# Down stage of a hybrid encoder block: four scratch half tiles are allocated ahead of the first four residual tiles

## The chip, the cores and the metric

The kernel runs on one core of a Trainium2 chip. The time of a run is device microseconds of that core, from one launch that computes the whole block. Beside the times there is one profiled execution, whose trace gives start, duration and releaser of each instruction on TensorE (PE for the matmuls, PEld for the weight loads), VectorE (DVE), ScalarE (ACT), GpSimd (POOL) and the DMA queues that SyncE (SP), ACT and POOL feed.

## The reference: what is computed

One layer of a streaming encoder over 1024 frames of width 1024, with 16 meta tokens ahead of them: a mixer (attention with a forgetting bias beside a diagonal state space model), and then a gated convolutional FFN, each with a residual, and a last norm.

```python
h = h + _mixer(_rmsnorm(h, norm_mix_g), ...)
xn  = _rmsnorm(h, norm_ffn_g)
hid = xn @ w_up                                   # 1024 -> 2 * 2816
conv = conv_b + sum(hp[:, j:j + L] * conv_w[j] for j in range(3))
val, gate = split(conv, 2)
h = h + (silu(gate) * val) @ w_down               # 2816 -> 1024: the Down stage
out = _rmsnorm(h, norm_final_g)[:, 16:]
```

Only the last product with its residual and the final norm lie behind the place of the change. The change leaves every number of it as it is.

## The kernel before, in words

**Up stage.** The hidden features come in 22 pairs of 128 rows, c = 0 to 21. For each pair the matmuls give a value half and a gate half; ACT and DVE apply the convolution into the tiles `ov` (value) and `og` (gate), 128 x 1024 floats each, ACT applies the silu to `og`, and one multiply (line 1313) puts the product into `ov`, which line 1320 stores to the DRAM array `a_d`. For c up to 20 the tiles are taken from two `ov` slots and one `og` slot, the multiply is POOL's and the store is issued by SP. For the last pair, c = 21, the two tiles are taken from the slots with the tag `h` (function `conv_out`), the multiply is DVE's and the store goes out on ACT's queue. The `hid` pool that holds all of these lies on the right side of SBUF and is closed at line 1755.

**Down stage.** `silu(gate) * val` times `w_down` is done as a Strassen-like scheme with seven products p = 0 to 6 on half matrices. The 11 row blocks of the inner dimension are dealt into four groups g = 0 to 3, of 2, 3, 3 and 3 blocks. `forms(p, j)` loads (SP, lines 1551, 1558, 1563) and splits the operands of one product and block into a high and a low part: a cast on ACT (line 1583) and a subtraction on POOL or DVE (line 137). `product(g, p, ...)` runs three matmuls (lines 1697 to 1699) per block into each of four PSUM banks, one for each token tile t = 0 to 3. Products 4, 5 and 6 add into the banks of products 0, 1 and 3 (`JOINS`): a bank is copied out after the first of the two, and again after the second. There are two sets of four banks, `mm, mm, mm, po` and `sp, tp, sp, tp`.

Of the first group, product 0 is copied out by ACT into four scratch half tiles `u2[0..3]`, 128 x 512 floats (line 1702). Product 4 goes on in the same four banks, and DVE adds these into the left halves of the residual tiles `hs[0..3]`, 128 x 1024 floats (line 1707). So PE may write product 4 into bank t only when ACT has copied it into `u2[t]`, and a later product may start on that bank only when DVE has added it into `hs[t]`. Products 1 and 5 of the first group are copied by ACT into `hs[4..7]` (line 1705). The residual rows themselves are loaded into `hs[0..3]` by four loads of 512 KB on SP's queue (line 1769), in a row; SP goes on with the operand loads of the next group behind them.

**Where the tiles lie.** After line 1755 the pool `down` is opened on the left side, and its tiles are laid out in the order in which they are asked for. They cover addresses that tiles of the closed pools held, and the framework makes the first write to a new tile wait for the last use of whatever lay there, tile by tile. In the built program, in bytes of a partition: the last pair's `ov_14620` lies at 164992 to 169104 and its `og_14527` at 169120 to 173232; the `ov` slots of the other pairs at 156800 to 160896 and 160896 to 164992; their `og` slot at 152704 to 156800. Before the change `hs0` to `hs3` fill 150240 to 166624 and `u20` to `u23` (the four `u2` tiles) 166624 to 174816.

The order of the instructions on each engine is set by a scheduler in the framework when the program is built. On each engine and each DMA queue they are issued in that order.

Of the kernel before, what the change touches and what calls it, by code (L numbers as in the profile page):

```python
# [9 lines left out]
F = mybir.dt.float32  # L10
# [9 lines left out]
P = 128  # L20
# [38 lines left out]
def block_kernel(ctx, tc, x, meta, xbt, x0t, g1t, w_q, w_k, w_v, w_f, w_u, w_g, b_f, w_ao, lam_d, bw_d, cw_d,  # L59
# [7 lines left out]
    def pool(stack, name, bufs=1, side=None, **k):  # L67
        return stack.enter_context(
            tc.tile_pool(name=name, bufs=bufs, side=side, reuse_waits="tile", **k))
# [1153 lines left out]
    u2 = [t_[:, i] for t_ in u2t for i in range(2)]  # L1223
# [532 lines left out]
    dn = pool(ctx, "down", side="left")  # L1756
# [3 lines left out]
    sq = dn.tile([P, 512], BF, name="sq")  # L1760
    eps = dn.tile([P, 1], F, name="eps")
    V.memset(eps, EPS)
    hs = [dn.tile([P, D], F, name=f"hs{c}") for c in range(4)]
    u2 = [dn.tile([P, 512], F, name=f"u2{c}") for c in range(4)]
    hs += [dn.tile([P, D], F, name=f"hs{c}") for c in range(4, KD)]
    small2 = [dn.tile([P, 4, 512], R, name=f"op{q}") for q in range(4, 6)]
    ops += [[t_[:, w] for w in range(4)] for t_ in small2]
# [420 lines left out]
```

## Time and profile before

| | us |
|---|---|
| median of 3 runs | 1429.18 (1429.15 to 1431.81) |
| the profiled execution, whole | 1430.84 |
| span of its trace | 1429.0 |
| PE busy | 1411.4 (99%) |
| POOL busy | 763.7 (53%) |
| DVE busy | 1068.9 (75%) |
| ACT busy | 708.8 (50%) |
| first matmul of the Down stage | 1205.42 |

A view "waits" lists who waited for whom on an engine, with the total, the number and the longest. "Timeline" lists instructions in order of time: start, duration, engine, line, operation, tiles, and in brackets the idle time of the engine just before and what ended it. "Windows" gives busy time by engine in stretches of the span, with the TensorE clock that was granted. "DMA" lists what was issued in a stretch, with the size and the median time from the issue to the landing. Times in the text are microseconds from the span's start.

### The profile page before, as it was taken

How to read it: one execution, taken by the hardware profiler on the slowest of the kernel's cores; microseconds unless marked ns; L12 is line 12 of the kernel's file. 1: busy time of each engine (PE TensorE's matmuls, PEld its weight loads, DVE VectorE, ACT ScalarE, POOL GpSimd, SP SyncE). 2: the span in 40 equal slices, each digit the busy share in tenths (PEclk: the TensorE clock that was granted, in tenths of full speed). 3: DMA queues.
4: the chain of work that ended last, by engine and by line, in shares of the span. 5: the costliest groups of instructions: out<-in, count | busy, mean ns of one | idle time of the engine just before them, and what ended most of it. 6: DMA issues, size and time to landing. Idle time of an engine off the chain costs nothing.

```text
span 1429.0 us, 26319 instructions
## 1 busy us (share of the span) xinstructions
PE 1411.4 (99%) x9607; PEld 1336.1 (94%) x9607; DVE 1068.9 (75%) x2048; ACT 708.8 (50%) x1381; POOL 763.7 (53%) x872
## 2 busy tenths in 40 slices
PE   8999999999999999999999999999999999999997
PEld 8999999988999999999889999999999999788886
DVE  7999888843667675665579977888887775698867
ACT  7647575423555565534645444444444445643444
POOL 1542267642456556327671344554546544798795
PEclk9999999999999999999999999999999999999999
DMA  8685744530157531087953246766644327864443
GB/s 301 174 200 144 157 111 137 165 119 31 53 156 168 127 103 56 24 302 274 195 169 125 68 126 162 201 183 173 167 127 133 98 83 274 282 209 129 132 94 118
DMA packets 93318, 216.17 MB, mean 151 GB/s; under 512 B 14802, under 2 KB 22610, under 8 KB 92804
## 3 DMA queue, kind: packets, MB, share of 16 engines
q1 hardware_dynamic: 74340, 170.28, 36.5%
q0 software_dynamic: 17696, 41.29, 15.0%
q10 hardware_dynamic: 1152, 2.91, 0.6%
q8 instruction: 76, 1.25, 0.4%
q14 instruction: 54, 0.44, 0.1%
HBM read 170.88 MB, written 71.71 MB: 170 GB/s over the span
## 4 chain that ended last, share of the span: by engine, by line
PE 94%; DMA 3%; ACT 1%; SPq 0%; DVE 0%; issue 0%; POOL 0%; POOLq 0%; DVEq 0%; ACTq 0%
PE mm L174 5%; PE mm L176 5%; PE mm L175 5%; PE sp L237 4%; PE sp L236 4%; PE sp L238 4%; PE tp L236 3%; PE mm L236 3%; PE tp L237 3%; PE mm L238 3%; PE tp L238 3%; PE mm L237 3%; PE po L966 3%; PE tp L920 2%; PE mm L1699 2%; PE mm L1697 2%
## 5 line engine op out<-in xcount | busy, mean ns | idle before, releaser
L174 PE MATMUL mm<-xhi,whi 128*128 128x342 f32 (+2 forms) x480 | 156.1, 325 | 0.0
L175 PE MATMUL mm<-xlo,whi 128*128 128x342 f32 (+2 forms) x480 | 155.3, 324 | 0.0
L176 PE MATMUL mm<-xhi,wlo 128*128 128x342 f32 (+2 forms) x480 | 154.7, 323 | 0.6 <-DMA wlo<-in_w_g_dram 0.6
L1313 POOL TENSOR_TENSOR ov<-ov,og 128x1024 f32<-128x1024 f32 x21 | 50.8, 2419 | 119.6 <-ACT og L1312 117.2
L137 DVE TENSOR_TENSOR sw<-sf,sw 128x512 fp32r<-128x512 f32 x72 | 73.4, 1019 | 45.8 <-ACT sw L1304 45.7
L1304 ACT CAST sw<-sf 128x512 fp32r<-128x512 f32 x72 | 44.9, 624 | 109.4 <-POOL sf L1451 79.9
L176 PEld LDWEIGHTS mm<-xhi,wlo 128*128 128x128 f32 x480 | 90.4, 188 | 1.6 <-DMA wlo<-in_w_g_dram 1.1
L174 PEld LDWEIGHTS mm<-xhi,whi 128*128 128x128 f32 x480 | 90.4, 188 | 1.1 <-issue 0.6
L175 PEld LDWEIGHTS mm<-xlo,whi 128*128 128x128 f32 x480 | 90.4, 188 | 0.4
L1451 POOL TENSOR_TENSOR sf<-raw,sf 128x512 f32<-128x512 f32 x36 | 62.8, 1744 | 38.8 <-DVE sw L137 38.6
L1451 POOL TENSOR_TENSOR sf<-raw 128x512 f32<-128x512 f32 x36 | 49.0, 1361 | 60.3 <-DVE sw L137 24.3
L238 PE MATMUL mm<-xhi,sw 128*128 128x258 f32 (+1 forms) x288 | 81.0, 281 | 0.0
L236 PE MATMUL mm<-xhi,sw 128*128 128x258 f32 (+1 forms) x288 | 80.8, 280 | 0.0
L237 PE MATMUL mm<-xlo,sw 128*128 128x258 f32 (+1 forms) x288 | 80.7, 280 | 0.0
L883 ACT ACTIVATE pt<-pt,mx 128x400 f32<-128x400 f32 (+5 forms) x72 | 53.1, 737 | 44.8 <-DVE mx L876 44.4
L1503 DVE SCALAR_TENSOR_TENSOR ov<-hv,cwt,ov 128x1024 f32<-128x1024 f32 x36 | 69.4, 1927 | 0.4 <-ACT ov L1501 0.4
L885 POOL TENSOR_SCALAR pt<-pt,mx 128x400 f32<-128x400 f32 (+5 forms) x72 | 51.8, 720 | 33.2 <-DVE mx L884 28.3
L1304 ACT CAST sw<-raw 128x512 fp32r<-128x512 f32 x70 | 43.0, 621 | 45.4 <-PE sp L238 23.5
L137 DVE TENSOR_TENSOR sw<-raw,sw 128x512 fp32r<-128x512 f32 x70 | 57.9, 830 | 4.2 <-ACT sw L1304 4.0
L137 DVE TENSOR_TENSOR tl<-tp,th 128x512 fp32r<-128x512 f32 (+1 forms) x80 | 50.7, 634 | 12.0 <-ACT th L923 11.3
L923 ACT CAST th<-tp 128x512 fp32r<-128x512 f32 (+1 forms) x80 | 43.4, 543 | 32.2 <-PE tp L920 22.5
L852 POOL CAST qz<-q 64x128 fp32r<-64x128 f32 (+1 forms) x72 | 20.2, 282 | 68.8 <-PE sp L871 67.4
(722 smaller groups left out, 5726.4 us busy)
## 6 DMA issues: line engine op xcount, KB each, us to landing
raw<-in_w_up_dram SPq DMA_DIRECT2D x44, 512.0 KB, 3.7
t_d<-in_w_dn_dram POOLq DMA_DIRECT2D x44, 256.0 KB, 7.1
wr<-t_d SPq DMA_DIRECT2D x44, 256.0 KB, 3.7
ar<-a_d SPq DMA_DIRECT2D x41, 256.0 KB, 4.3
a_d<-ov SPq DMA_DIRECT2D x18, 512.0 KB, 2.6
wr<-in_w_dn_dram SPq DMA_DIRECT2D x33, 256.0 KB, 3.8
t_d<-in_w_dn_dram SPq DMA_DIRECT2D x22, 256.0 KB, 4.3
t_d<-t_d SPq DMA_DIRECT2D x22, 256.0 KB, 4.8
```

The lines of the kernel that those rows point to most:

```text
L137: return eng.tensor_tensor(out_, src, hi.bitcast(F), ALU.subtract)
L174: yield PE.matmul(ps, whi[:, i, :], ahi[:, i], start=(i == 0), stop=False)
L175: yield PE.matmul(ps, whi[:, i, :], alo[:, i], start=False, stop=False)
L176: yield PE.matmul(ps, wlo[:, i, :], ahi[:, i], start=False, stop=(i == k - 1))
L236: PE.matmul(ps, a[0][:, i], bh, start=(i == 0 and not joins), stop=False, skip_group_check=True)
L237: PE.matmul(ps, a[0][:, i], bl, start=False, stop=False, skip_group_check=True)
L238: PE.matmul(ps, a[1][:, i], bh, start=False, stop=(i == kh - 1), skip_group_check=True)
L883: ends[:] = rd, S.activation(pt[:n, :kc], pt[:n, :kc], AF.Exp, bias=low, scale=-1.0, accum_out=nm[:n, 0:1])
L885: sc_.append(GP.tensor_scalar(pt[:n, :kc], pt[:n, :kc], nm[:n, 1:2], 1.0, ALU.mult, ALU.mult))
L1304: S.copy(hi, src)
L1451: sums.append(GP.tensor_tensor(f_, a, b, op))
L1503: V.scalar_tensor_tensor(out=o, in0=h_[:, j:SEQ + j], scalar=cwc(j, m), in1=o, op0=ALU.mult, op1=ALU.add)
```

## The change

Two lines trade places: the four `u2` tiles are asked for ahead of `hs[0..3]`.

```diff
     eps = dn.tile([P, 1], F, name="eps")
     V.memset(eps, EPS)
+    u2 = [dn.tile([P, 512], F, name=f"u2{c}") for c in range(4)]
     hs = [dn.tile([P, D], F, name=f"hs{c}") for c in range(4)]
-    u2 = [dn.tile([P, 512], F, name=f"u2{c}") for c in range(4)]
     hs += [dn.tile([P, D], F, name=f"hs{c}") for c in range(4, KD)]
     small2 = [dn.tile([P, 4, 512], R, name=f"op{q}") for q in range(4, 6)]
```

The addresses then are: `u20` to `u23` at 150240 to 158432, `hs0` at 158432 to 162528, `hs1` at 162528 to 166624, `hs2` at 166624 to 170720, `hs3` at 170720 to 174816. All else lies where it lay. The number in a tile's name is given in the order of asking, so `u20_14762` becomes `u20_14758`, and `hs0_14758` becomes `hs0_14762`.

No engine's instructions stand in another order than before; what differs is what some of them wait for. The names in brackets below are semaphores: `PE_49`, `DVE_49`, `Pool_49` and `Activation_49` count an engine's finished instructions, `DMAHW0_49` to `DMAHW7_49` landed transfers; on ACT and SP below `DMAHW5_49` is that of the last pair's store, `a_d<-ov_14620`.

On ACT, at the turn from the Up to the Down stage (`mm`, `po` are PSUM banks, `ar` and `wr` loaded operands, `xlo` a place for split ones):

```order
 L1361 ACTIVATE ov_14620<-mm_14677,cwt_9030 128x340 [waits PE_49]
 L1320 DMA a_d_81<-ov_14620 128x1024 [waits DVE_49]
-L1702 COPY u20_14762<-mm_14792 128x512 [waits DMAHW5_49,PE_49]
-L1702 COPY u21_14763<-mm_14793 128x512 [waits PE_49,Activation_49]
-L1702 COPY u23_14765<-po_14795 128x512
+L1702 COPY u20_14758<-mm_14792 128x512 [waits PE_49]
+L1702 COPY u21_14759<-mm_14793 128x512 [waits PE_49,Pool_49]
+L1702 COPY u23_14761<-po_14795 128x512
 L1583 CAST xlo_98<-ar_14870 128x512 [waits DMAHW1_49]
 L1583 CAST xlo_98<-wr_14868 128x512 [waits DMAHW0_49]
```

The first copy no longer waits for the store of the last pair; the second waits for POOL, which multiplied the pair before the last.

On SP's queue, at the residual loads, with the first operand loads of the next group behind them:

```order
-L1769 DMA hs0_14758<-h_d_80 128x1024 [waits DMAHW6_49]
-L1769 DMA hs1_14759<-h_d_80 128x1024 [waits DMAHW7_49]
-L1769 DMA hs2_14760<-h_d_80 128x1024 [waits DMAHW0_49]
-L1769 DMA hs3_14761<-h_d_80 128x1024 [waits DMAHW5_49,DMAHW1_49,DVE_49]
+L1769 DMA hs0_14762<-h_d_80 128x1024 [waits DMAHW6_49,DMAHW0_49]
+L1769 DMA hs1_14763<-h_d_80 128x1024 [waits DMAHW7_49,DMAHW5_49,DVE_49]
+L1769 DMA hs2_14764<-h_d_80 128x1024
+L1769 DMA hs3_14765<-h_d_80 128x1024 [waits DMAHW1_49]
 L1558 DMA ar_14916<-a_d_81 128x512 [waits DMAHW2_49]
 L1558 DMA ar_14918<-a_d_81 128x512 [waits DMAHW3_49,PE_49]
```

The wait for the last pair's store moves from the fourth residual load to the second; `hs2`, `hs3` and all operand loads stand behind it.

On DVE, the first adds of the Down stage, which read the banks and the residual tiles, and the splits behind them:

```order
-L1707 TENSOR_TENSOR hs0_14758<-hs0_14758,mm_14792 128x512 [waits DMAHW6_49,PE_49,Pool_49]
-L1707 TENSOR_TENSOR hs1_14759<-hs1_14759,mm_14793 128x512 [waits DMAHW7_49,PE_49]
-L137 TENSOR_TENSOR xlo_98<-ar_14886,xlo_98 128x512 [waits DMAHW5_49]
+L1707 TENSOR_TENSOR hs0_14762<-hs0_14762,mm_14792 128x512 [waits DMAHW0_49,DMAHW6_49,PE_49,Pool_49]
+L1707 TENSOR_TENSOR hs1_14763<-hs1_14763,mm_14793 128x512 [waits DMAHW5_49,DMAHW7_49,DVE_49,PE_49]
+L137 TENSOR_TENSOR xlo_98<-ar_14886,xlo_98 128x512
 L137 TENSOR_TENSOR xlo_98<-wr_14884,xlo_98 128x512 [waits DMAHW4_49]
 L137 TENSOR_TENSOR xlo_98<-ar_14894,xlo_98 128x512
 L137 TENSOR_TENSOR xlo_98<-wr_14892,xlo_98 128x512
```

The adds stand where they stood; the second one's residual tile now is the one that is loaded behind the store.

## The prediction

> **What bounds the kernel now.** The first part of the page and the view of PE's waits come first:
>
> ```profile
> PE 1411.4 (99%) x9607; PEld 1336.1 (94%) x9607; DVE 1068.9 (75%) x2048; ACT 708.8 (50%) x1381; POOL 763.7 (53%) x872
> ...
> PE mm L355 <- ACT uh L413: 5.3, 1, 5.3
> PE mm L1697 <- ACT u L1702: 2.7, 1, 2.7
> PE mm L176 <- DMA wlo<-in_w_g_dram: 0.6, 1, 0.6
> ```
>
> PE is the bound nearly everywhere, so a change pays only where PE stands still. Past the start of the program it does so in one place worth the name: 2.7 us at line 1697 for the copy of line 1702, the copy out of product 0 into `u2`. So the next view is ACT's timeline, to see why that copy is late:
>
> ```profile
> 1211.32 0.33 ACTq L1320 DMA_DIRECT2D a_d<-ov  x1
> 1218.52 1.07 ACT L1702 COPY u<-mm 128x512 f32<-128x512 f32 x2 [9.76 <-DMA a_d<-ov]
> 1219.47 0.60 ACT L1702 COPY u<-po 128x512 f32<-128x512 f32 x1
> ...
> 1226.50 0.68 ACT L1583 CAST op<-ar 128x512 fp32r<-128x512 f32 x1
> 1227.02 0.68 ACT L1583 CAST xhi<-ar 128x512 fp32r<-128x512 f32 x1
> ```
>
> ACT issues the last pair's store at 1211.32, and then stands in front of its first copy until the store has landed, for no reason but that `u20` lies on the bytes that are being stored. The copy's data had long been there, and PE's own timeline shows what it cost:
>
> ```profile
> 1209.97 0.39 PE L1699 MATMUL mm<-op 128*128 128x512 f32 x1
> ...
> 1214.95 0.39 PE L1697 MATMUL mm<-op 128*128 128x512 f32 x1
> ...
> 1216.09 0.39 PE L1699 MATMUL mm<-op 128*128 128x512 f32 x1
> 1219.15 0.50 PE L1697 MATMUL mm<-op 128*128 128x512 f32 x1 [2.68 <-ACT u L1702]
> ...
> 1220.42 0.61 PE L1699 MATMUL mm<-op 128*128 128x512 f32 x1
> ...
> 1223.82 0.41 PE L1698 MATMUL po<-op 128*128 128x512 f32 x1
> ...
> 1224.99 0.40 PE L1697 MATMUL mm<-xhi 128*128 128x512 f32 x1
> ...
> 1226.36 0.39 PE L1697 MATMUL mm<-xhi 128*128 128x512 f32 x1
> ```
>
> The last matmul of product 0 in the three banks that ACT copies first starts at 1209.97. Six matmuls of the fourth bank run from 1214.95 to 1216.09, five steps of 0.228 us. Then comes the gap, and the matmuls from 1220.42 to 1223.82 take 3.40 us for eight steps, 0.425 each. The windows say why:
>
> ```profile
> 1216.00:1219.20 3.20, 0.52 (x4) 0.10 (x2) 0.00 (x0) 0.69 (x2) 0.00 (x0) 1.00 0.04 15
> 1220.40:1223.80 3.40, 3.40 (x9) 2.65 (x8) 0.86 (x2) 3.40 (x8) 3.13 (x3) 0.50 0.99 348
> ...
> 1240.00:1260.00 20.00, 20.00 (x89) 16.46 (x88) 18.63 (x22) 9.10 (x18) 20.00 (x13) 1.00 0.77 258
> ```
>
> The number behind the five engines is the granted clock: 0.50 in the 3.4 us that follow the gap, 1.00 around it. The gap is paid for a second time.
>
> **What the change takes away.** From 1216.09 to 1224.99 PE makes 19 steps. At 0.228 us they are 4.33 us; they took 8.90. The whole loss is 4.57 us. Of it the half clock is 3.40 - 8 x 0.228 = 1.58 us, and the gap with its slow first steps the other 2.99.
>
> With the new addresses the first copy waits for PE alone, the second for POOL's multiply of the pair before, which was over before the store of that pair was issued at 1198.42 (row below). So the three copies can run from 1211.7, right behind the issue of the store (1211.32 + 0.33), and end at about 1213.2 (1.07 for two, 0.6 for one). PE wants the first at 1216.3. That leaves 3 us of cover, and if it were gone only the part beyond it would come back. No instruction, byte or copy is added.
>
> **Where the wait goes.** It goes to SP's queue: the second residual load now stands behind the store, with `hs2`, `hs3` and the operand loads of the next group queued behind it. What they waited for before:
>
> ```profile
> SPq L1769 <- DMA a_d<-ov: 10.8, 1, 10.8
> ...
> 1198.42 0.32 SPq L1320 DMA_DIRECT2D a_d<-ov  x1
> ...
> 1206.27 12.56 SPq L1769 DMA_DIRECT2D hs<-h_d  x4
> 1218.51 0.32 SPq L1769 DMA_DIRECT2D hs<-h_d  x1
> 1218.88 3.91 SPq L1558 DMA_DIRECT2D ar<-a_d  x6
> 1219.83 0.43 SPq L1558 DMA_DIRECT2D ar<-a_d  x1
> ...
> a_d<-ov SPq DMA_DIRECT2D x18, 512.0 KB, 2.6
> a_d<-ov SPq DMA_DIRECT2D x1, 512.0 KB, 3.0
> a_d<-ov ACTq DMA_DIRECT2D x1, 512.0 KB, 7.1
> hs<-h_d SPq DMA_DIRECT2D x1, 512.0 KB, 6.8
> hs<-h_d SPq DMA_DIRECT2D x2, 512.0 KB, 10.4
> hs<-h_d SPq DMA_DIRECT2D x1, 512.0 KB, 3.7
> ar<-a_d SPq DMA_DIRECT2D x1, 256.0 KB, 5.1
> ...
> 1210.00:1214.00 4.00, 4.00 (x19) 3.34 (x18) 1.26 (x3) 0.00 (x0) 0.00 (x0) 1.00 0.93 365
> ```
>
> These are SP's waits, its timeline, and DMA views: the page's store line, then single stretches: the store of 1198.42 (3.0), the last store (7.1), the first residual load (6.8), the third (10.4), the fourth (3.7), and the third operand load (5.1). The fourth residual load (1218.51) was behind the store before, and with it the operand loads, of which the third was issued at 1219.83. Three things differ now.
>
> First, the store's own landing, which no row shows without the two other residual loads in front of it. They keep the DMA engines 93% busy at 365 GB/s from 1210 to 1214, and the store took 7.1 us. Now only `hs0`, issued five microseconds earlier, is in front. The bounds are 2.6 us (the other stores) and 7.1. I take 3.0, the store after a quiet stretch, since one load is not three: landing at 1214.3.
>
> Second, `hs1`. Issued at 1214.4, it lands 3.7 us later by the lone fourth load, at 1218.1; the bounds are 3.7 and 10.4, the latter among three loads at once. DVE wants it when PE has ended product 4 in bank 1, which without the stall is 1216.32 + 11 x 0.228 + 0.39 = 1219.2. So it costs nothing, and there is more room yet: before, DVE's add of 1223.63 ended 2.0 us ahead of the matmul at 1226.36 that reuses the bank.
>
> ```profile
> 1223.63 0.69 DVE L1707 TENSOR_TENSOR hs<-hs,mm 128x512 f32<-128x512 f32 x1 [1.81 <-PE mm L1699]
> ...
> 1257.38 0.67 DVE L1707 TENSOR_TENSOR u<-u,tp 128x512 f32<-128x512 f32 x1
> ...
> 1220.67 1.29 POOL L137 TENSOR_TENSOR xlo<-ar,xlo 128x512 fp32r<-128x512 f32 x1 [22.28 <-PE mm L1698]
> ...
> 1227.26 1.80 POOL L137 TENSOR_TENSOR op<-ar,op 128x512 fp32r<-128x512 f32 x1 [1.11 <-ACT op L1583]
> 1229.02 1.84 POOL L137 TENSOR_TENSOR xhi<-ar,xhi 128x512 fp32r<-128x512 f32 x1
> ...
> 1258.46 0.39 PE L1697 MATMUL tp<-op 128*128 128x512 f32 x1
> ```
>
> Third, the operand loads. They are issued at about 1215.7 instead of 1218.88, 3.2 us earlier, but with 1 MB more of residual tiles ahead, at 365 GB/s 2.9 us; they land 0.3 us earlier than before, or 0.4 more at the pace of the fourth load's neighbours. This is the tight place, for POOL has hardly a break from 1227.26 on (20.00 of 20 in the last window above), and its chain ends in DVE's add at 1257.38, which is over 0.41 us before PE needs the bank at 1258.46. POOL's second step, at 1229.02, needs the third operand load, which landed at 1219.83 + 5.1 = 1224.9 and will land at 1224.2 to 1224.6; with the cast (0.68) POOL can start at 1224.9 to 1225.3. To keep PE's whole gain it would have to start at 1229.02 - 4.57 = 1224.45. The shortfall of 0.4 to 0.9 less the 0.41 of slack leaves 0 to 0.5 us. I take 0: from 1227.26 on POOL's steps ran at 1.8 us with DVE busy beside it, against the 1.29 of 1220.67, and the splits ahead of DVE's adds now come where POOL is idle.
>
> **The sum.** The profiled execution took 1430.84 us (span 1429.0). Without the 4.57 us it takes 1426.27. The median of the runs shown is 1429.18, 1.66 below the profiled one, nearly the 1.58 of the half clock. So I read the median runs as runs whose gap did not fall so that the clock was halved: they lose 2.99 us, and come to 1426.2 as well. If they did have the half clock, and the 1.66 is the profiler's, 4.57 goes off 1429.18: 1424.6.
>
> [...]
>
> **The rivals.** *The operands become the wait.* The store lands as late as it did, at 1218.4, because what slows it is not the load in front. Then `hs1` comes at 1222.2, its add ends at 1222.9, and PE, which wants bank 1 at 1216.32 + 24 x 0.228 = 1221.8, stands 1.1 us. Worse, the operand loads are as late as before plus 2.9 us for the two tiles ahead: the third at 1227.8, POOL's second step at 1228.5, 0.5 earlier than before instead of 4.57. PE then meets DVE's add of 1257.38 with a gain of 0.5 + 0.41 = 0.9: 1429.9 against the profiled run, 1429 against the median. For it: the same 7.1 us. Against it: eighteen other stores at 2.6.
>
> *The residual loads crawl.* The loads issued from 1206.27 took 6.8 to 10.4 us. If the store is late and the three behind it are as slow, `hs3` lands at 1228.9 and the third operand load about 2.1 us behind it (three times 256 KB at 365 GB/s), at 1231.0; POOL's second step starts at 1231.7, 2.7 later than before, and PE, past its 0.41 of slack, ends 2.3 later: 1433.1, slower. It decides as soon as the third operand load lands later than 1225.3. Against it: the fourth load took 3.7.
>
> *It does nothing.* If something else held the first copy, PE still waits until 1219: 1429.2. ACT's row says that only the landing released it, and that wait is gone from the copy.
>
> **How the numbers follow.** The wait goes and nothing takes its place: 78%, of it 46 at 1426.2 (up to 0.5 more by the POOL shortfall) and 32 at 1424.6. Operands become the wait, or a part of it: 14%, 1427 to 1430. Crawling loads: 5%, 1433.1. Nothing: 3%, 1429.2. The forecast is 1426.2 us. The range 1424.3 to 1428.4 takes in both readings of the clock and the milder half of the first rival, and leaves out the rest. About 0.2%, 2.86 us, is what a measurement of this kernel can tell from no change, so faster means below 1426.3: all of the 32 and just over half of the 46, 0.57. Within: 0.38. Slower: 0.05.
>
> **What would show it.** In the new profile PE's wait at line 1697 for `u` is gone, the copies of line 1702 start near 1211.7, the granted clock stays 1.00 from 1216 to 1226, and the matmul of 1224.99 starts at about 1220.4. The store's landing time is near 3 us, and the second residual load is issued near 1214.4. I am wrong if the store still takes about 7 us, if PE waits for DVE at the adds of line 1707 near 1222 or 1254, or if the median drops by 4.5, which would say that the half clock was in every run.

## The result, and the profile after

The changed kernel takes **1426.95 us** (median of 17 runs, 1425.53 to 1428.47), the kernel before 1429.49 beside it (17 runs, 1427.21 to 1432.34). The ratio is 0.9981, with a 95% interval of 0.9974 to 0.9989: 2.5 us off, by the interval 1.6 to 3.7. The forecast was 1426.2 with a range of 1424.3 to 1428.4; it had given 0.57 to a time below 1426.3, and the time is above that. The profiled executions differ by more, 1430.84 against 1427.24, and that difference between 2.5 and 3.6 is what the experiments below are about.

The engines' line and PE's waits of the kernel after:

```profile
PE 1410.6 (99%) x9607; PEld 1336.1 (94%) x9607; DVE 1070.3 (75%) x2048; ACT 709.0 (50%) x1381; POOL 764.2 (54%) x872
...
PE mm L355 <- ACT uh L413: 5.2, 1, 5.2
PE mm L1208 <- DVE olo L137: 0.6, 1, 0.6
PE mm L176 <- DMA wlo<-in_w_g_dram: 0.5, 1, 0.5
```

PE's wait at line 1697 for `u` is gone, and nothing of the Down stage has taken its place in the list. ACT's timeline of the kernel after shows why:

```profile
1212.54 0.33 ACTq L1320 DMA_DIRECT2D a_d<-ov  x1
1212.90 1.08 ACT L1702 COPY u<-mm 128x512 f32<-128x512 f32 x2 [2.94 <-DVE eps L1762]
1213.87 0.60 ACT L1702 COPY u<-po 128x512 f32<-128x512 f32 x1
...
1222.06 0.62 ACT L1583 CAST op<-ar 128x512 fp32r<-128x512 f32 x1 [1.00 <-DMA ar<-a_d]
1223.48 0.62 ACT L1583 CAST xhi<-ar 128x512 fp32r<-128x512 f32 x1 [0.80 <-DMA ar<-a_d]
```

The copies follow right behind the issue of the last pair's store. (The 2.94 us in brackets began before that issue, when ACT stood for DVE's multiply of the last pair, which ended at 1212.51; the name `eps` beside it is only the instruction of DVE that came next.) The last two casts of the row now wait for their operands, 1.00 and 0.80 us. Before, they waited for ACT's own queue. PE's timeline and one window of the kernel after (behind the length stand the busy times of PE, PEld, DVE, ACT and POOL, the granted clock, the DMA share and GB/s):

```profile
1206.63 0.40 PE L1697 MATMUL mm<-op 128*128 128x512 f32 x1
...
1217.30 0.39 PE L1699 MATMUL mm<-op 128*128 128x512 f32 x1
1217.52 0.39 PE L1697 MATMUL mm<-op 128*128 128x512 f32 x1
...
1221.60 0.39 PE L1697 MATMUL mm<-xhi 128*128 128x512 f32 x1
...
1216.00:1224.00 8.00, 8.00 (x37) 6.64 (x36) 4.24 (x6) 6.20 (x13) 5.31 (x5) 1.00 0.95 353
```

Where the gap stood (1217.30 to 1217.52 here) the step is 0.22 us, and the clock stays at 1.00. Times of two executions are compared from the first matmul of line 1697 on, here 1206.63, before 1205.42; this is the zero of all offsets below. The matmul named in the prediction comes 14.97 us after it, where it came 19.57 after it before: 4.60 us. Last matmul less first is 210.43 against 215.18 us, 4.75 shorter. Since the Down stage began 1.2 us later in this execution, the totals differ by 3.6.

SP's wait and queue, DVE's add of `hs1`, POOL's second step, and the landing of the store and of the third operand load (issued at 1217.49) in the kernel after:

```profile
SPq L1769 <- DMA a_d<-ov: 7.2, 1, 7.2
...
1215.20 1.27 SPq L1769 DMA_DIRECT2D hs<-h_d  x3
1216.52 2.94 SPq L1558 DMA_DIRECT2D ar<-a_d  x6
...
1220.44 0.69 DVE L1707 TENSOR_TENSOR hs<-hs,mm 128x512 f32<-128x512 f32 x1 [0.61 <-PE mm L1699]
...
1224.18 1.62 POOL L137 TENSOR_TENSOR xhi<-ar,xhi 128x512 fp32r<-128x512 f32 x1
...
a_d<-ov ACTq DMA_DIRECT2D x1, 512.0 KB, 2.6
ar<-a_d SPq DMA_DIRECT2D x1, 256.0 KB, 5.9
```

SP stands 7.2 us for the store, and it costs nothing. The store lands 2.6 us after its issue, `hs1` is issued at 1215.20, and DVE's add of `hs1` at 1220.44 waited for PE alone, so the tile was there within 5.2 us. POOL's second step begins 17.55 us after the zero (23.60 before).

### The profile page after: what moved, and what is told of

Same layout as the page of the kernel before. It is cut to its first block, busy times and chain, and to the rows that moved or that the text cites. A ratio compares the mean times of both kernels' runs of the same rounds, so it can differ in the third digit from the quotient of the medians.

```text
span 1425.5 us, 26319 instructions
## 1 busy us (share of the span) xinstructions
PE 1410.6 (99%) x9607; PEld 1336.1 (94%) x9607; DVE 1070.3 (75%) x2048; ACT 709.0 (50%) x1381; POOL 764.2 (54%) x872
## 4 chain that ended last, share of the span: by engine, by line
PE 95%; DMA 2%; issue 1%; ACT 1%; DVE 0%; POOL 0%; POOLq 0%; DVEq 0%; SPq 0%
PE mm L174 5%; PE mm L176 5%; PE mm L175 5%; PE sp L236 4%; PE sp L237 4%; PE sp L238 4%; PE tp L236 3%; PE tp L237 3%; PE tp L238 3%; PE mm L238 3%; PE mm L236 3%; PE mm L237 3%; PE po L966 3%; PE tp L920 2%; PE mm L1699 2%; PE mm L1698 2%
```

## The experiments

All kernels issue the same instructions in the same order on every engine as the kernel before; only the order in which the Down stage's pool hands out addresses differs, and with it who waits for the last pair's store and what stands ahead of that store in the queues. The offsets are from the first matmul of line 1697, worked out from the rows of each trace. The first four were timed beside 33 runs of the kernel before (1428.21), the next two beside 21 (1428.97). The six rows at the end of the table are one more profile each of a kernel from above.

| kernel | store lands after | step at the gap | half clock | POOL's second step | second stall | stage, first to last matmul | median, ratio (95%) |
|---|---|---|---|---|---|---|---|
| before (first profile) | 7.1 | 3.07 | 3.41 us | 23.60 | none | 215.18 | 1429.49 |
| after | 2.6 | none | no | 17.55 | none | 210.43 | 1426.95, 0.9981 (0.9974 to 0.9989) |
| copy2_waits | 7.3 | 1.87 | no | 23.16 | 0.84, 1.51 | 214.56 | 1430.41, 1.0011 (1.0002 to 1.0020) |
| copy3_waits | 4.9 | none | no | 20.22 | 1.12 | 211.66 | 1426.72, 0.9986 (0.9977 to 0.9995) |
| copy_waits_store_early | 2.6 | none | no | 19.13 | none | 210.44 | 1426.02, 0.9982 (0.9973 to 0.9991) |
| four_loads_in_front | 7.1 | 3.07 | no | 23.49 | 1.39 | 214.73 | 1430.67, 1.0017 (1.0009 to 1.0026) |
| all_clear | 7.1 | none | no | 19.81 | none | 210.51 | 1426.55, 0.9982 (0.9973 to 0.9990) |
| all_loads_behind | 2.6 | none | no | 18.79 | none | 210.44 | 1426.67, 0.9984 (0.9975 to 0.9993) |
| before_again_1 | 5.5 | 1.49 | no | 21.91 | 1.38 | 213.38 | one profile, 1429.53 |
| before_again_2 | 5.0 | 0.94 | no | 21.34 | 2.51 | 213.70 | one profile, 1428.25 |
| before_again_3 | 5.6 | 1.59 | no | 22.00 | 1.33 | 213.21 | one profile, 1429.45 |
| before_again_4 | 5.4 | 1.36 | no | 21.77 | 1.38 | 213.00 | one profile, 1427.61 |
| four_loads_again_1 | 6.9 | 2.81 | no | 23.22 | 1.41 | 214.47 | one profile, 1429.41 |
| four_loads_again_2 | 7.4 | 3.32 | 6.83 us | 23.39 | none | 216.49 | one profile, 1431.59 |

"Step" and "stall" are from one matmul's start to the next, of which 0.23 us is the usual step. "Stage" is the Down stage. In all of these traces the store is issued 5.90 us into it.

**One wait left, on the second copy.** `u21` lies on the store instead of `u20`:

```
-    hs = [dn.tile([P, D], F, name=f"hs{c}") for c in range(4)]
+    hs = [dn.tile([P, D], F, name=f"hs{c}") for c in range(0, 3)]
     u2 = [dn.tile([P, 512], F, name=f"u2{c}") for c in range(4)]
-    hs += [dn.tile([P, D], F, name=f"hs{c}") for c in range(4, KD)]
+    hs += [dn.tile([P, D], F, name=f"hs{c}") for c in range(3, KD)]
```

> The u2 tiles are asked for behind hs0, hs1 and hs2, so that the second copy (u21), not the first, lies on the last pair's store, and three residual loads stay in front of that store as before. Counted from the first matmul of the Down stage (D): the store lands at D + 13.0 as before, PE wants the second bank at D + 12.3 and stands about 1.4 us. My theory (PE pays for the time that a copy waits for the store, and the half clock only if the gap fills enough of a clock window): 1.6 us slower than the changed kernel, about 1428.5 us, 1.4 below before; half clock in few runs. Rival (any wait of a copy for the store brings the half clock): 3.2 us slower than the changed kernel, about 1430.1. Rival (the gain came from the first copy alone): as the changed kernel, 1427.0.

The condition under which the half clock comes, in the first theory, was the author's estimate; the rows on it stand with the last of the experiments. PE's waits of this kernel and ACT's row:

```profile
PE mm L1697 <- ACT u L1702: 1.5, 1, 1.5
PE tp L1697 <- DVE u L1707: 1.1, 1, 1.1
PE mm L1697 <- DVE u L1707: 0.5, 1, 0.5
...
1217.85 0.59 ACT L1702 COPY u<-mm 128x512 f32<-128x512 f32 x1 [6.30 <-DMA a_d<-ov]
```

The first wait of 1.5 us was foreseen; the two waits for DVE behind it were not, and so the median is 1430.41 and not 1428.5. It lies near the 1430.1 of the first rival, but not by that rival's cause: the profile has no half clock in the stage. The stage is 4.1 us longer than after the change, and the kernel is a little slower than before. The address of one copy, with three residual loads again in front of the store, thus gives back the whole gain, and more than its own gap.

**One wait left, on the third copy.** The same edit with `range(0, 2)` and `range(2, KD)`: `u23` lies on the store.

> The u2 tiles are asked for behind hs0 and hs1: the third copy (u23) lies on the last pair's store, and two residual loads are in front of the store. The store lands between D + 8.5 (one load in front) and D + 13.0 (three), about D + 11; PE wants that bank at D + 13.6. My theory: no gap, as the changed kernel within 0.4 us (about 1427.0), with ACT held for about 3 us that nobody waits for. Rival (ACT's casts and copies behind the held copy become the wait): 1 to 2 us slower than the changed kernel.

```profile
1211.60 0.33 ACTq L1320 DMA_DIRECT2D a_d<-ov  x1
1211.96 1.08 ACT L1702 COPY u<-mm 128x512 f32<-128x512 f32 x2 [2.94 <-DVE eps L1762]
1216.50 0.59 ACT L1702 COPY u<-po 128x512 f32<-128x512 f32 x1 [3.46 <-DMA a_d<-ov]
```

That is ACT's timeline. ACT is held until 1216.50, the third bank's copy is in time for PE, and there is no gap. With two residual loads ahead the store took 4.9 us. Yet ACT's casts behind the copy are late, and PE stands 0.9 us beyond its usual step at the later place (the stall of 1.12 in the table). In the timed runs this 0.9 us can't be told from the changed kernel (0.9986 and 0.9981, each with an interval of 0.0009 or less to a side); beside copy_waits_store_early, the next experiment, which was timed together with it, the median is 0.7 us longer (1426.72 against 1426.02), which would fit.

**All copies still wait, but the store is early.** `u20` lies on the store as before, and the second residual load stands behind it:

```
-    hs = [dn.tile([P, D], F, name=f"hs{c}") for c in range(4)]
+    hs = {}
+    hs.update((c, dn.tile([P, D], F, name=f"hs{c}")) for c in (4, 5, 0, 1))
     u2 = [dn.tile([P, 512], F, name=f"u2{c}") for c in range(4)]
-    hs += [dn.tile([P, D], F, name=f"hs{c}") for c in range(4, KD)]
+    hs.update((c, dn.tile([P, D], F, name=f"hs{c}")) for c in (2, 3, 6, 7))
```

> The first copy lies on the last pair's store as in the kernel before, but hs1 does too, so that only hs0 is loaded in front of the store, as in the changed kernel. My theory: the store lands 2.6 to 3 us after its issue, at D + 8.5 to 8.9, the first copy runs at D + 8.6 to 9.0, PE wants the bank at D + 10.9, no gap: as the changed kernel within 0.4 us (1427.0), though the copy waits for the same store as before. Rival (the wait itself costs, whatever the store takes): as before, 1429.5.

Its ACT timeline:

```profile
1210.62 0.33 ACTq L1320 DMA_DIRECT2D a_d<-ov  x1
1213.30 1.08 ACT L1702 COPY u<-mm 128x512 f32<-128x512 f32 x2 [5.26 <-DMA a_d<-ov]
```

The copies wait for the very same store, and the whole gain is there: 210.44 us, 0.9982. A wait of the copies for the store cost nothing by itself here (210.43 us in the changed kernel); it cost where the store landed 5.0 to 7.4 us after its issue (stages of 213.00 to 216.49 us).

**Four loads in front.** The residual loads ahead of the store are four instead of three:

```
-    hs = [dn.tile([P, D], F, name=f"hs{c}") for c in range(4)]
+    hs = {}
+    hs.update((c, dn.tile([P, D], F, name=f"hs{c}")) for c in (0, 1, 2, 4))
     u2 = [dn.tile([P, 512], F, name=f"u2{c}") for c in range(4)]
-    hs += [dn.tile([P, D], F, name=f"hs{c}") for c in range(4, KD)]
+    hs.update((c, dn.tile([P, D], F, name=f"hs{c}")) for c in (3, 5, 6, 7))
```

> The first copy lies on the last pair's store as before, and none of the four residual loads does, so all four go out in front of the store or beside it, and SP's operand loads with them. My theory: the store lands at D + 14.4 or later, PE stands 4 us or more at the first bank and the half clock follows in nearly every run: 5.5 to 8 us slower than the changed kernel, 1432.5 to 1435, that is 3 to 5 slower than before. Rival (what delays the store is not the loads in front of it): as before, 1429.5.

The store came no later than in the first profile of the kernel before (7.1 us), against what was expected, though three operand loads of 256 KB were issued ahead of it too (2.87 to 4.97 us into the stage); the stage is 4.3 us longer than after, not 5.5 to 8. The gap is the same 3.07 as in that profile, and no half clock follows it. PE's waits:

```profile
PE mm L1697 <- ACT u L1702: 2.7, 1, 2.7
PE tp L1697 <- DVE u L1707: 1.0, 1, 1.0
```

In place of the half clock stands a second wait, for DVE's add of `u`, 52.6 us into the stage.

**The store late, but nobody on PE's path waits for it.** The `u2` tiles first, then `hs0`, then the pair of operand tiles, so that an operand load meets the store:

```
-    hs = [dn.tile([P, D], F, name=f"hs{c}") for c in range(4)]
     u2 = [dn.tile([P, 512], F, name=f"u2{c}") for c in range(4)]
-    hs += [dn.tile([P, D], F, name=f"hs{c}") for c in range(4, KD)]
+    hs = [dn.tile([P, D], F, name=f"hs{c}") for c in range(0, 1)]
     small2 = [dn.tile([P, 4, 512], R, name=f"op{q}") for q in range(4, 6)]
+    hs += [dn.tile([P, D], F, name=f"hs{c}") for c in range(1, KD)]
```

> u2 is asked for first, then hs0, then the two operand tiles op4 and op5, which come to lie on the last pair's tiles, then the other residual tiles: neither a copy nor a residual load waits for the last pair's store. My theory (in the changed kernel the wait on SP's queue is hidden): the same as the changed kernel within 0.4 us, 1427.0, with the operand loads landing some 3 us earlier for nothing. Rival (that wait costs something): up to 0.5 us faster than the changed kernel.

SP's wait and ACT's timeline:

```profile
SPq L1558 <- DMA a_d<-ov: 7.4, 1, 7.4
...
1212.12 1.08 ACT L1702 COPY u<-mm 128x512 f32<-128x512 f32 x2 [2.94 <-DVE eps L1762]
...
1218.96 0.62 ACT L1583 CAST op<-ar 128x512 fp32r<-128x512 f32 x1 [3.21 <-DMA a_d<-ov]
```

The store takes 7.1 us again, SP stands 7.4 us for it, ACT 3.21 at a cast, and PE loses nothing (210.51). Together with copy_waits_store_early this says: either the store early or the copies free of it is enough, and no more is to be had by both.

**All loads behind the store.** `u2` first, then `hs4` and `hs0`, so that even the first residual load waits:

```
+    hs = {}
     u2 = [dn.tile([P, 512], F, name=f"u2{c}") for c in range(4)]
+    hs.update((c, dn.tile([P, D], F, name=f"hs{c}")) for c in (4, 0, 1, 2, 3, 5, 6, 7))
```

> u2 is asked for first, and hs0 to hs3 all stand behind the last pair's store on SP's queue, with the operand loads behind them. My theory: the store lands at D + 8.5, hs0 at D + 12.3, just before DVE wants it at D + 12.5; the third operand load lands about 1.3 us later than in the changed kernel, at D + 18.1, and POOL's second step starts at D + 18.9, against the D + 19.0 that PE needs: 0 to 0.4 us slower than the changed kernel, 1427.0 to 1427.4. Rival (the operands become the wait): 1 to 2 us slower, 1428 to 1429.

The stage is 210.44 us, as after the change. The moved wait still has room, as expected: `hs0` is issued 8.66 us into the stage instead of 0.89, POOL's second step comes 1.2 us later, and PE does not meet it. No residual load at all is in front of the store here, and it lands after the same 2.6 us as behind one.

**The kernel before, four more times, and the four loads twice more.** These are kernels from above as they were, profiled for the half clock and the second stall.

> The kernel before, unchanged, profiled once more, for its gap and its clock: the time of the 17 runs spreads over 5 us, that of the changed kernel over 3. My theory: a gap at the first copy in every execution, 2 to 4 us with the landing of the store, and the half clock behind it in some and not in others. Rival: gap and half clock are the same each time, and the spread comes from the start of the program.

> The same as the run before this one, a third profile of the kernel before: the store lands 5 to 8 us after its issue, the gap is 1 to 4 us, and the granted clock is 0.50 behind it where the gap is 2 us or more.

> The kernel before, unchanged, once more with a profile, to see how often its gap at line 1697 is followed by the half clock and how often by a second stall at DVE's u adds of line 1707. Theory (a gap of any length over 1 us delays the casts and the POOL chain, so that PE meets the adds again some 38 us later unless the half clock has already given the chain that time): first matmul to last matmul of the Down stage is 213.4 to 215.2 us; either a granted clock of 0.50 for 3.4 us behind the gap and no second stall, or full clock and a second stall of 1 to 2.3 us near 51 us after the first matmul. Rival (the second stall has nothing to do with the gap): it comes with the half clock too, or does not come without it, and the stage is then 212 or 217 us.

> As for before_again_3. The store lands 5.0 to 7.1 us after its issue in the three profiles so far; both theories expect it within that.

In none of the four is there a half clock in the stage. The store lands after 5.0 to 5.6 us, and the gap is 0.7 to 1.4 us beyond the usual step, less than the 2 to 4 that were expected of the first of them. In each of the four PE stands a second time, as the theory of before_again_3 has it; the stage of before_again_3 and that of before_again_4 are 0.2 and 0.4 us under the 213.4 that it gave as the least. Of before_again_1, PE's waits, then ACT, POOL, DVE and PE:

```profile
PE mm L1697 <- ACT u L1702: 1.1, 1, 1.1
PE tp L1697 <- DVE u L1707: 1.0, 1, 1.0
...
1217.49 1.07 ACT L1702 COPY u<-mm 128x512 f32<-128x512 f32 x2 [8.19 <-DMA a_d<-ov]
1218.45 0.60 ACT L1702 COPY u<-po 128x512 f32<-128x512 f32 x1
...
1225.48 0.68 ACT L1583 CAST op<-ar 128x512 fp32r<-128x512 f32 x1
1226.01 0.68 ACT L1583 CAST xhi<-ar 128x512 fp32r<-128x512 f32 x1
...
1227.89 1.84 POOL L137 TENSOR_TENSOR xhi<-ar,xhi 128x512 fp32r<-128x512 f32 x1
...
1256.27 0.68 DVE L1707 TENSOR_TENSOR u<-u,tp 128x512 f32<-128x512 f32 x1
...
1255.62 0.39 PE L1699 MATMUL sp<-xhi 128*128 128x512 f32 x1
1257.00 0.50 PE L1697 MATMUL tp<-op 128*128 128x512 f32 x1 [0.99 <-DVE u L1707]
```

From the first copy to the cast of `xhi` ACT works 8.5 us without a break, so that cast, and POOL's step behind it, are late by what the copy is late. DVE's add is then too late for PE, at the very matmul which the prediction had found with 0.41 us to spare. By the prediction's rows that add ends 29.03 us after POOL's second step begins (1229.02 to 1257.38 + 0.67), and without any stall PE wants the bank at 48.43 (1255.06 in the trace after, less 1206.63). So a stall of (POOL's second step + 29.03) less (48.43 + what PE has lost so far) should follow. For before_again_1 that is 50.94 - 49.87 = 1.07, with 1.15 found; for before_again_3 and before_again_4 1.06 and 1.09 (1.10 and 1.15 found); four_loads_in_front 1.10 (1.17); four_loads_again_1 1.11 (1.18); copy2_waits 1.23 (1.28); copy3_waits 0.82 (0.89); for the first profile of before, after, copy_waits_store_early, all_loads_behind and four_loads_again_2 none (none found). It misses twice: before_again_2 1.09 (2.28 found), and all_clear 0.41 (none found). In all_clear the add ended 28.46 us after POOL's second step and not 29.03, at 48.28, and so in time. In before_again_2 it ended 30.16 after it, and the traces show where the 1.1 us went. Here are a split that DVE makes between two adds of this chain, and POOL's step beside it, in before_again_1 and then in before_again_2:

```profile
1252.27 0.68 DVE L137 TENSOR_TENSOR xlo<-wr,xlo 128x512 fp32r<-128x512 f32 x1
1252.26 1.83 POOL L1574 TENSOR_TENSOR ar<-ar 128x512 f32<-128x512 f32 x1
...
1250.07 1.83 DVE L137 TENSOR_TENSOR xlo<-wr,xlo 128x512 fp32r<-128x512 f32 x1
1250.07 1.29 POOL L1574 TENSOR_TENSOR ar<-ar 128x512 f32<-128x512 f32 x1
```

The split took 1.15 us longer, and POOL's step, which started with it, 0.54 less; in the other thirteen traces the two took 0.68 and 1.82 to 1.85. Why it went the other way once isn't shown.

> Four residual loads ahead of the last store, once more, for the half clock. If the half clock follows every gap of about 2.7 us, it is there now and was missed by a hair in the first profile of this kernel; if it depends on where the gap falls in windows that run free of the kernel, it comes in some of these profiles and not in others with the same gap. Store landing about 7.1 us after issue, gap of 2.7 us at line 1697; Down stage 214.7 us without the half clock (with a second stall of 1.0), 215.2 with it (without the second stall).

> As for four_loads_again_1: a gap of 2.7 us at line 1697 that is followed by the half clock in each profile by the one theory, in some of them by the other; Down stage 214.7 us or 215.2.

Here one profile has no half clock and a stage of 214.47 us, and the other has it for 6.83 us, twice the 3.41 of the first profile of before, and then no second stall; its stage is 216.49 and not 215.2. In the first profile of before the clock records last 1211.73 us at 1.00, 3.413 at 0.50 and 201.39 at 1.00, and in that of after the first lasts 1409.70 at 1.00: 355, 1, 59 and 413 times 3.413. Counted on in such steps, a boundary falls 1.3 us into the Down stage in before and 2.2 in after. In stretches of that length, laid by the clock records of each trace, the rows are, for before (the gap, the half clock), four_loads_in_front, four_loads_again_1, and four_loads_again_2 (the gap, the half clock in two stretches, and the one behind):

```profile
1217.01:1220.42 3.41, 1.27 (x6) 1.05 (x6) 0.00 (x0) 1.91 (x4) 0.00 (x0) 1.00 0.22 42
1220.42:1223.83 3.41, 3.41 (x10) 2.67 (x9) 0.89 (x2) 3.41 (x8) 3.16 (x3) 0.50 0.99 350
```

```profile
1214.27:1217.68 3.41, 2.38 (x11) 1.65 (x9) 0.00 (x0) 0.00 (x0) 0.00 (x0) 1.00 1.01 369
1217.68:1221.09 3.41, 1.76 (x8) 1.45 (x9) 0.01 (x1) 2.40 (x5) 0.24 (x1) 1.00 0.45 172
```

```profile
1214.21:1217.62 3.41, 1.61 (x8) 0.99 (x6) 0.00 (x0) 0.02 (x1) 0.00 (x0) 1.00 0.99 390
```

```profile
1214.67:1218.08 3.41, 1.31 (x6) 0.75 (x4) 0.00 (x0) 0.00 (x0) 0.00 (x0) 1.00 0.91 356
1218.08:1221.49 3.41, 2.57 (x6) 2.11 (x7) 0.00 (x0) 3.21 (x7) 1.06 (x1) 0.50 0.28 97
1221.49:1224.91 3.42, 3.42 (x9) 2.68 (x9) 1.16 (x2) 3.42 (x8) 3.42 (x4) 0.50 0.63 173
1224.91:1228.32 3.41, 3.41 (x16) 2.78 (x16) 3.41 (x5) 2.55 (x6) 1.78 (x3) 1.00 0.74 224
```

The second column of times is PE's. In before and in four_loads_again_2 the stretch that is followed by the half clock has PE busy for 1.27 and 1.31 us. In four_loads_again_1 the clock stays at 1.00 behind one with 1.61, and in four_loads_in_front behind 2.38 and 1.76. The step at the gap is 3.07 us both in before and in four_loads_in_front, and the half clock follows in before alone; so between these two traces it was not the length of the gap that decided. Of the 2.7 us, 2.14 lie in one stretch in before, and in four_loads_in_front they are cut 1.03 and 1.65. That this made the difference is the author's reading of these four traces. In the four later profiles of before PE's wait at the gap is 0.5 to 1.2 us, so that a stretch of 3.41 has PE busy for 2.2 or more (2.31 in before_again_1), and no half clock follows. In four_loads_again_2 the clock stays at 0.50 behind the stretch with 2.57 us busy and is at 1.00 behind the next, with 3.42; in before it is at 1.00 behind the one with 3.41.

## Why the prediction was right, and where it was not

**The change and its first effect: right.** The wait at line 1697 is gone, the copies run from 1212.90, 0.36 us behind the store's issue at 1212.54, the clock stays at 1.00, and PE's matmul comes 4.60 us earlier where 4.57 were worked out for that execution. That the address was the cause is shown from both sides: copy2_waits puts one copy back on the store and the loss is back; all_clear leaves the store as late as it was and there is no loss.

**The store: right.** 3.0 us was taken, between 2.6 and 7.1; it was 2.6. That the loads in front delay it is shown by no load in front (2.6, all_loads_behind), one (2.6, after and copy_waits_store_early), two (4.9) and three or four (5.0 to 7.4). The one load of the kernel after had landed 0.15 us after the store was issued (issued at 0.89 and landed at 6.05 of the stage, the store issued at 5.90), so there it was hardly in front any more.

**The moved wait: right.** `hs1` was in time, SP's wait of 7.2 us costs nothing, and POOL's shortfall was taken at 0 out of 0 to 0.5: its second step had to begin by 19.03 (1224.45 of the profile before), and began at 17.55. Two readings on the way were wrong. The casts before it had been thought to wait for the operand load; the rows quoted in the prediction (1226.50 and 1227.02 follow one another with no wait) say that in the kernel before ACT's own queue held them. And the load was put too late: the 1 MB of residual tiles ahead of it was priced at 2.9 us, but the third operand load took 5.9 us where it had taken 5.1, only 0.8 more, and was issued 3.5 us earlier in the stage and not 3.2. It landed at 16.8 of the stage, against 18.8 to 19.2 foreseen. That is why POOL gained 6.05 us and not the 3.7 to 4.1 that its start at 1224.9 to 1225.3 would have been, and why no shortfall came.

**The size in the median runs: the number held, its parts did not.** The forecast takes 2.99 us off the 1429.18 of the runs shown, as a gap of full length without the half clock, and reads the 1.66 us between the profiled run and the median as the half clock's 1.58. This is the term that was mis-sized. Without the half clock the gap was not 2.84 us beyond the usual step but 0.7 to 1.4 in four profiles of the kernel before, since the store landed after 5.0 to 5.6 us and not 7.1; the profile it was sized from is the only one of five with the long landing. And a term is missing: the second stall at DVE's add, 1.1 us in three of them and 2.3 in the fourth. The prediction had priced that stall as a rival that the change might bring in, and not seen that the kernel before has it in each of the four profiles without the half clock: the half clock and the long gap of that one execution delayed PE by so much that DVE's add was just in time, the 0.41 us of slack. The sum of the two in those profiles is 2.3 to 3.0 us, and with the slower steps behind the gap the stage is 2.6 to 3.3 us longer than after. The medians say 2.5, 2.2 to the best of the first four variants and 2.4 to the better of the next two. That 2.99 came close to it is thus in part luck. The second reading, a half clock in every run and 1424.6, fell.

**The rivals.** "The operands become the wait" did not come with the change, but its second half, POOL's chain and DVE's add, is real: it was there before the change, and copy2_waits and copy3_waits have it. It comes by ACT's queue, not by SP's. "The residual loads crawl" and "it does nothing" fell: `hs1`, the load behind the store, was there within 5.2 us of its issue, and PE's wait at the copy is gone.

**What stays open.** Why the store lands at 5.0 to 5.6 us in four executions of the kernel before and at 7.1 in one, with the same three loads in front. How often timed runs have the half clock is shown in part, by the mean granted clock that each of them left. In the fourteen profiles it is 0.997 and 0.996 in the two with the half clock in the stage, and 0.998 or 0.999 in the others. Of the 54 timed runs of the kernel before that stood beside the experiments one has 0.997 (1430.12 us) and none has less; of the eleven of four_loads_in_front six have 0.996 or 0.997, among them the five slowest (1431.81 to 1432.35). So the half clock seems to be seldom in the kernel before, though not surely as seldom as this: 3.41 us at half are 0.0012 of the mean, and some of the runs at 0.998 can hide one. At the start of the program there is no clock record until 8.69 us in the first profile of before and 10.80 in that of after. PE's pace changes there: equal matmuls of 128x272 start 0.23 us apart from 5.73 on in before and 0.13 from 8.82 on, and in after 0.23 from 5.63 on and 0.13 from 11.21 on. That the clock is half until then is the author's estimate from this pace. The Down stage began at 1204.4 to 1206.6; a part of the 3 to 5 us by which the timed runs of one kernel differ would lie there, ahead of anything this change touches.

## What to carry to other kernels

When a copy is released by a landing, look not only at who waits for that copy, but at all that is queued behind it on its engine without a break: here 8.5 us of ACT's work carried the delay to a second stall 39 us on. Size a stall by several profiles before its cause is priced, above all where it hangs on a transfer behind others: the same kernel had a gap of 0.7 to 2.8 us. An address can cost in two ways, by the wait and by what that wait lets run ahead of the transfer; here either remedy alone, the copies free of the store or the store early, was worth the whole gain, so one is enough.

## What the runs showed of the hardware

- A store of 512 KB landed 2.6 us after its issue with no residual load of 512 KB in front of it or one that had landed or all but landed when it was issued, 4.9 with two, and 5.0 to 7.4 with three or four, on queues of different engines.
- The granted TensorE clock was 0.50 in the Down stage for 3.41 us in the first profile of before and for 6.83 in four_loads_again_2, each time behind 3.41 us in which PE was busy for 1.27 and 1.31; none of the other twelve profiles had it in the stage. It stayed at 1.00 behind 3.41 us with 1.61 busy (four_loads_again_1) and with 1.76 and 2.38 (four_loads_in_front). In four_loads_again_2 it stayed at 0.50 behind 2.57 us busy and was 1.00 behind 3.42, in before behind 3.41.
- In those two profiles with the half clock the second stall was absent, and the whole loss was 4.8 and 6.1 us, where the others with a gap had 2.6 to 4.3.
- Of two steps that DVE and POOL started at the same time, DVE's took 0.68 us and POOL's 1.82 to 1.85 in thirteen traces, and 1.83 and 1.29 in one.
